# Two blocks on one core: keys' parts share the partitions, splits on VectorE, routing in steps

## The chip, the core and the metric

The kernel runs on one core of a Trainium2 chip. A core has five engines that work at the same time, each through its own list of instructions in a fixed order: TensorE (PE: matrix products; PEld is its loading of the stationary operand), VectorE (DVE), ScalarE (ACT), GpSimd (POOL) and SyncE (SP). SP and POOL also issue DMAs. An instruction waits on semaphores for what it needs, and everything behind it on that engine waits too. The metric is the device time of one execution in microseconds (us); three runs of the kernel before took 2537.84 to 2539.66, median 2538.1.

## The reference

Two blocks follow one another on 1024 rows of width 1024, in float32. The first projects x by a wide matrix and feeds three branches (gated spatial mixing, an S5 state-space scan with parameters computed from small tensors, cross attention to a memory), joins them by an output product and a layer norm. The second makes an RG-LRU recurrence and a differential attention beside one another, then a second memory attention and a mixture of 32 experts, of which each row takes two:

```python
def second_block(x, mem, positions, ...):
    h = rms_norm(x, norm_mix)
    lru_in, lru_gate, q, k, v, g_lru, g_attn = split(h @ w_in)
    y_lru = (gelu(lru_gate) * rg_lru(conv(lru_in))) @ w_lru_o
    # q, k: 8 heads, 2 maps of 64; v: 128 per head; mask by chunks of 64 keys
    q, k = rope(rms_norm(q)) / 8, rope(rms_norm(k))
    sc = einsum('bqhmd,bkhd...->bhmqk', q, k)
    p = softmax(where(mask, sc, -1e30));  w = p[:, :, 0] - lam * p[:, :, 1]
    y_attn = rms_norm(w @ v) @ w_attn_o
    x = x + (sigmoid(g_lru) * y_lru + sigmoid(g_attn) * y_attn) @ w_out
    x = x + memory_cross_attention_2(x, mem)            # 4 heads of 128
    hf = rms_norm(x)                                    # group, then 2 of its 8 experts
    for expert e, rows of it: x += weight * (silu(hf @ gate_e) * (hf @ up_e)) @ down_e
```

## The kernel before, in words

**Products.** A float32 product is made of three matmuls on halves: each operand is split into a rounded high part (`wh`, `xh`, written by ACT, L154) and the rest (`wl`, `xl`, a subtraction on DVE or POOL, L166); `mm3` (L174 to L176) adds high by high, low by high and high by low. Weights come by DMA into `raw`, are split, and are held in rings of two to four buffers.

**Block 1** (`block1`, 0 to about 375 us) begins with eight slices of x (`xraw`, 128x1024 each) and the weight `w_gx`; each slice is split as it lands, most low parts on DVE and every third on POOL, and the first product (tile `pj`) takes one slice after the other. In its own `weights` (L471) the low part goes to POOL. In the same time DVE computes the S5 parameters, a chain of some hundred small instructions (`par_*`, `C`, `S`, `pw`, `ang`). Three lanes, the S5 scan with gating (`left`), the memory attention (`attend`) and the plain projections (`dense`), are merged by a clock of estimated costs.

**Attention** (`attention`, 723 to 1484 us) goes over four pairs of heads. A pair has 16 units: 8 query tiles of 128 rows by 2 heads. For a unit, `unit_qk` makes the scores of both maps in PSUM (`sc`), `unit_mix` the softmax (ACT exponent `e`, DVE), `unit_tr` transposes the weights (`pt<-ident,e`), `unit_pv` multiplies with the values `V`. To keep PE busy, `fill` steps through a generator of other work between units: projections of keys and values (`k_tiles`), of queries (`q_tile`), and gates (`gate_unit`); PSUM products of 24 matmuls of 256 columns. A key tile is normed and rotated (`nr`, on DVE, in a ring of three), twice side by side so that 4 transposes give the same 64 values on both halves of the partitions; `kh` and `kl` are its parts. A query tile `qs` has its high part on partitions 0 to 63 and its low part on 64 to 127, so that one matmul with `kh` and one with `kl` cover all four products. The mask is one more matmul per map, of 256 columns in fp32r (L1482). There is one buffer of `kh`, `kl`, `V`, so at the end of a pair the keys and values of the next are made with no unit beside them (`nxt` stays empty there, and `need` runs the generator).

**Mixer and routing** (`mixer_tiles`, 1642 to 1922 us): the second memory attention in steps s1 to s10 for eight row tiles, each step one tile behind the other; s8 ends x2 and makes the router's rows `h`, s9 transposes them, s10 makes the logits `plg`. `route` chooses experts and fills the lists `lst`, for tiles 0 to 3 early, and for (4, 5, 6) and then (7,) one after the other at the end. A gather of rows by `lsti` starts the experts.

**Experts** (`moe`, 1922 us to the end): PE makes for each expert four groups of 12 matmuls of 512 columns (`pg`, up and gate) and two (`pd`, down), the weights streaming in by DMA, 1 MB each, split in ACT and DVE instructions of 128x2048. `moe_order` and the scheduler set in which order ACT and DVE interleave these with the small steps: `tg` (gating), `xh`, `xl` and `ah`, `al` (inputs of the products), `y` (output, then scattered to memory by POOL, L2213). `beyond`, once, finds the rows that don't fit the 96 of an expert.

Of the kernel before, what the change touches and what calls it, by code (L numbers as in the profile page):

```python
# [30 lines left out]
NY = 3  # L31
# [98 lines left out]
class Model:  # L130
# [321 lines left out]
    def block1(self):  # L452
# [18 lines left out]
        def weights(src, shape, tag, bufs=2, eng=nc.gpsimd):  # L471
# [13 lines left out]
        with tc.high_priority(3 * URGENT):  # L485
            w_gx = weights(A["w_gx"][0], [128, 8, 128], "d", 2, None)
            for k in range(8):
                if 4 <= k < 6:
                    raw = W.tile([128, 1024], F32, name="xraw", tag="wr", bufs=2)
                else:  # L490
                    raw = S5.tile([128, 1024], F32, name="xraw", tag=("u0", "u1", "k", "yt")[k % 4])
# [224 lines left out]
        def attend():  # L716
# [6 lines left out]
            for t in (kph, kpl, vph, vpl):  # L723
                nc.gpsimd.memset(t.bitcast(F32), 0.0)
# [199 lines left out]
        for z in Gx + BT:  # L924
            nc.gpsimd.memset(z.bitcast(F32), 0.0)
# [240 lines left out]
    def attention(self):  # L1166
# [4 lines left out]
        with self.pool("at1") as T1, self.pool("at") as T, \  # L1171
# [16 lines left out]
            ma = T.tile([128, 128], F32R, name="ma")  # L1188
            mb = T.tile([128, 384], F32R, name="mb")
            nc.gpsimd.memset(ma.bitcast(F32), 0.0)  # L1190
            nc.gpsimd.memset(mb.bitcast(F32), 0.0)
            nc.vector.memset(ma.bitcast(F32)[0:1, 0:64], 1.0)
            nc.vector.memset(mb.bitcast(F32)[0:1, 192:256], -(2.0 ** 100))
            self.at = (T, PS, PT, PJ, ma, mb, lamn, sub)

# [24 lines left out]
            def norm_rope(ps, i, is_k):  # L1220

                d = T1.tile([128, 4, 2, 64], F32, name="nr", tag="nr", bufs=3)
# [8 lines left out]
                if is_k:  # L1231
                    self.tt(d, ps[:, :, None, :].to_broadcast([128, 4, 2, 64]),
                            ss[:, 4:8, None, None].to_broadcast([128, 4, 2, 64]), OP.mult)
# [3 lines left out]
                for j in range(2):  # L1237
# [4 lines left out]
                self.tt(d[:, :, :, 0:16], r[:, 0, :, None, :].to_broadcast([128, 4, 2, 16]),  # L1242
                        r[:, 1, :, None, :].to_broadcast([128, 4, 2, 16]), OP.add)
                return d, ss[:, 4:8]

            def transposed(d):
# [1198 lines left out]
```

## Time and profile before

| | |
|---|---|
| median of three runs | 2538.1 us |
| profiled execution | 2542.32 us, of which the span of the trace 2540.4 |
| PE, PEld busy | 2381.8 us (94%), 1966.0 (77%) |
| DVE, ACT, POOL busy | 1775.6 us (70%), 1245.3 (49%), 594.0 (23%) |
| DMA | 394 MB, 155 GB/s over the span, 350 GB/s and more among the experts |

"Busy" counts time in which an instruction of the engine runs. PE's matmuls overlap: one of 512 columns lasts about 400 ns in the record, but the next starts 230 ns later, and one of 256 columns 285 ns with the next 118 ns later; so what a matmul costs is read from start to start. The chain of waits of this profile holds only the last scatter and says nothing of what came before; time is therefore read by stages.

### The profile page before, as it was taken

The numbers are of one execution on the slowest core, as the hardware profiler recorded it, in microseconds if no ns is written. First come the engines' busy times: TensorE is split into PE (matmuls) and PEld (weight loads), VectorE is DVE, ScalarE is ACT, GpSimd is POOL, SyncE is SP. The second block draws the span as 40 slices with busy tenths as digits, with TensorE's granted clock in tenths as the row PEclk, the third lists the DMA queues.
The fourth block names the chain that finished last, engine by engine and source line by source line (L and its number), as shares of the span: only waits on it lengthen the run. The fifth ranks groups of instructions, "written<-read, shape, count | busy, mean of one in ns | idle before, by whom it ended". The sixth has DMA issues, their size and how long they took to land. (4 is left out here: it accounts for less than half of the span.)

```text
span 2540.4 us, 34497 instructions
## 1 busy us (share of the span) xinstructions
PE 2381.8 (94%) x13016; PEld 1966.0 (77%) x13016; DVE 1775.6 (70%) x3153; ACT 1245.3 (49%) x1850; POOL 594.0 (23%) x425
## 2 busy tenths in 40 slices
PE   6999979998989999999999899999988998999997
PEld 5888868777889899898898778887876766766665
DVE  8567677687785676666666743334557998999897
ACT  4354532345455444545454532034435776776665
POOL 4322213222131021021021010001222232333343
PEclk9999989999999999999999999999998999999999
DMA  5322335322121101101110366541247997999995
GB/s 185 116 64 73 115 115 184 121 69 71 65 75 50 55 30 55 63 34 49 52 51 34 110 207 215 176 164 69 84 199 274 374 377 266 349 370 360 350 341 201
DMA packets 104281, 394.28 MB, mean 155 GB/s; under 512 B 14641, under 2 KB 33585, under 8 KB 79537
## 3 DMA queue, kind: packets, MB, share of 16 engines
q1 hardware_dynamic: 85584, 335.41, 37.0%
q0 software_dynamic: 18528, 56.65, 7.1%
q8 instruction: 104, 1.70, 0.3%
q14 instruction: 65, 0.52, 0.1%
HBM read 339.07 MB, written 61.31 MB: 158 GB/s over the span
## 5 line engine op out<-in xcount | busy, mean ns | idle before, releaser
L154 ACT ACTIVATE wh<-raw 128x2048 fp32r<-128x2048 f32 (+2 forms) x310 | 479.7, 1557 | 312.9 <-PE pj L175 82.2
L166 DVE TENSOR_TENSOR wl<-raw,wh 128x2048 fp32r<-128x2048 f32 (+2 forms) x287 | 553.4, 1939 | 96.3 <-ACT wh L154 95.8
L174 PE MATMUL pj<-wh,xnh 128*128 128x256 f32 x768 | 223.1, 290 | 8.9 <-ACT pc L154 4.7
L2213 POOL DMA_INDIRECT out<-y,lsti x32 | 145.9, 4559 | 356.3 <-DVE y L162 343.3
L176 PE MATMUL pj<-wh,xnl 128*128 128x256 f32 x768 | 218.5, 284 | 0.0
L175 PE MATMUL pj<-wl,xnh 128*128 128x256 f32 x768 | 217.8, 284 | 0.0
L175 PE MATMUL pg<-wl,xh 128*96 128x512 f32 x512 | 205.0, 400 | 13.3 <-DVE wl L166 12.6
L176 PE MATMUL pg<-wh,xl 128*96 128x512 f32 x512 | 201.8, 395 | 0.0
L174 PE MATMUL pg<-wh,xh 128*96 128x512 f32 x512 | 200.3, 397 | 0.0
L174 PEld LDWEIGHTS pj<-wh,xnh 128*128 128x128 f32 x768 | 145.8, 190 | 11.9 <-ACT pc L154 6.7
L179 POOL TENSOR_TENSOR ss<-ss,mhalf 128x4 f32<-128x4 f32 (+1 forms) x68 | 74.0, 1088 | 314.2 <-DVE ss L163 222.1
L175 PEld LDWEIGHTS pj<-wl,xnh 128*128 128x128 f32 x768 | 146.6, 191 | 0.0
L176 PEld LDWEIGHTS pj<-wh,xnl 128*128 128x128 f32 x768 | 145.4, 189 | 0.0
L154 ACT ACTIVATE e<-sc,st,ss 128x1024 f32<-128x1024 f32 (+7 forms) x128 | 105.6, 828 | 67.9 <-DVE st L158 50.9
L175 PEld LDWEIGHTS pg<-wl,xh 128*96 128x96 f32 x512 | 82.8, 162 | 55.8 <-DVE wl L166 23.2
L174 PEld LDWEIGHTS pg<-wh,xh 128*96 128x96 f32 x512 | 83.0, 162 | 37.2 <-ACT wh L154 2.2
L174 PE MATMUL pj<-xnh,wh 128*128 128x512 f32 x256 | 103.6, 405 | 5.6 <-ACT wh L154 5.6
L176 PEld LDWEIGHTS pg<-wh,xl 128*96 128x96 f32 x512 | 83.1, 162 | 33.0 <-DVE xl L166 0.2
L174 PE MATMUL pg<-xnh,wh 128*128 128x512 f32 x256 | 103.7, 405 | 0.0
L175 PE MATMUL pg<-xnl,wh 128*128 128x512 f32 x256 | 102.5, 400 | 0.0
L176 PE MATMUL pj<-xnh,wl 128*128 128x512 f32 x256 | 102.4, 401 | 0.0
L176 PE MATMUL pg<-xnh,wl 128*128 128x512 f32 x256 | 102.4, 400 | 0.0
(999 smaller groups left out, 6590.2 us busy)
## 6 DMA issues: line engine op xcount, KB each, us to landing
raw<-in_w_gu SPq DMA_DIRECT2D x128, 1024.0 KB, 9.0
raw<-in_w_dn SPq DMA_DIRECT2D x64, 1024.0 KB, 9.8
raw<-in_w_out SPq DMA_DIRECT2D x16, 512.0 KB, 4.4
ta<-tg POOLq DMA_DIRECT2D x32, 256.0 KB, 2.6
t<-ta SPq DMA_DIRECT2D x14, 512.0 KB, 4.2
raw<-in_w_ga SPq DMA_DIRECT2D x12, 512.0 KB, 3.8
raw<-in_w_v SPq DMA_DIRECT2D x12, 512.0 KB, 3.5
xraw<-in_xT SPq DMA_DIRECT2D x8, 512.0 KB, 6.4
```

What stands on the lines that cost most here:

```text
L154: return self.nc.scalar.activation(out=out, in_=in_, func=func, **kw)
L166: return (eng or self.nc.vector).tensor_tensor(out=out, in0=a, in1=b, op=op)
L174: mm(ps, l[0], r[0], start=start, stop=False)
L175: mm(ps, l[0], r[1], start=False, stop=False)
L176: mm(ps, l[1], r[0], start=False, stop=stop)
L179: self.nc.gpsimd.tensor_tensor(out=out, in0=in_, in1=self.mhalf[:, :w], op=OP.pow)
L2213: return nc.gpsimd.indirect_dma_start(out=self.out, out_offset=bass.IndirectOffsetOnAxis(ap=u["row"], axis=0), in_=u["y"], in_offset=None, ...
```

## The change

**Start.** The first weight and the slices of x get a higher priority than the small parameters; a seventh slice has a buffer of its own; all low parts in block 1 and the clearings of `kph`, `kpl`, `vph`, `vpl`, `Gh`, `Gl`, `Bh` and `Bl` (7424 columns in all) are on DVE, and a few small DMAs move from SP's queue to POOL's.

```diff
-        def weights(src, shape, tag, bufs=2, eng=nc.gpsimd):
+        def weights(src, shape, tag, bufs=2, eng=None):
-        with tc.high_priority(3 * URGENT):
+        with tc.high_priority(5 * URGENT):
-                self.split(xh[:, k], xl[:, k], raw, nc.gpsimd if k % 3 == 2 else None)
+                self.split(xh[:, k], xl[:, k], raw)
...
-                nc.gpsimd.memset(t.bitcast(F32), 0.0)
+                nc.vector.memset(t.bitcast(F32), 0.0)
...
-            nc.sync.dma_start(out=kd[u].rearrange("p g k n -> (p g k) n")[:, 0:7 * 16], in_=pad)
+            nc.gpsimd.dma_start(out=kd[u].rearrange("p g k n -> (p g k) n")[:, 0:7 * 16], in_=pad)
```

SP's list at the start of the kernel before, from its sixth row (`in_xT` are the slices of x, `in_w_gx` the weight, `kd`, `pos`, `lq`, `bc`, `cmat`, `dsk` small tensors; the last three stand ahead of these rows):

```order
L473 DMA raw<-in_w_gx 128x1024
L492 DMA xraw<-in_xT 128x1024 x6
L928 DMA kd_183<-pad 128x112
L928 DMA kd_184<-pad 128x112
L928 DMA kd_185<-pad 128x112
L928 DMA kd_186<-pad 128x112
L374 DMA pos<-in_pos 128x8
L407 DMA lq<-in_lamqk 128x256
L473 DMA raw<-in_w_gx 128x1024
L492 DMA xraw<-in_xT 128x1024 x2
L473 DMA raw<-in_w_xb 128x1024 x2
```

Here four small DMAs and two more stand between the sixth slice and the last two. SP's list after, from its third row:

```order
L473 DMA raw<-in_w_gx 128x1024
L491 DMA xraw<-in_xT 128x1024 x7
L270 DMA bc<-in_s5b 128x256
L272 DMA cmat<-in_s5c 128x256
L922 DMA dsk<-in_ssd 16x16
L374 DMA pos<-in_pos 128x8
L407 DMA lq<-in_lamqk 128x256
L473 DMA raw<-in_w_gx 128x1024
L491 DMA xraw<-in_xT 128x1024
L473 DMA raw<-in_w_xb 128x1024 x2
```

Seven slices now follow the weight directly; the parameters come behind them, and the eighth slice after the second weight.

**Attention.** Keys: the high part of a map lies on one half of the partitions and the low part on the other, in one tile `kk` with two buffers; `qs` holds the high and the low part on both halves. A key tile is no longer doubled, so it takes 2 transposes, not 4 (256 become 192 in all, with the queries'). The mask has 64 columns in bf16. The gates' result `tg` and the attention's output `ot`, which a DMA of POOL's queue stores, had a buffer each and now take theirs from the ring `nr`. The generator makes keys and values of the first pair first; then in each pair the queries and gates, the values `V` of the pair after its second query tile, and the keys of the next pair at its end, and the loop over units no longer stops between pairs.

```diff
-                kh = T.tile([128, 4, 1024], F32R, name="kh", tag="kh")
-                kl = T.tile([128, 4, 1024], F32R, name="kl", tag="kl")
...
+                kk = KV[p] = [T.tile([128, 4, 1024], F32R, name="kk", tag="kk", bufs=2), None]
-                    self.act(kh[:, :, q], pt, AF.Copy, scale=gcol[:, 1:2])
-                    self.stt(kl[:, :, q], pt, gcol[:, 1:2], kh[:, :, q].bitcast(F32), OP.mult, OP.subtract)
+                    for m in range(2):
+                        a, b = slice(64 * m, 64 * m + 64), slice(64 - 64 * m, 128 - 64 * m)
+                        g = gcol[a, 1:2]
+                        self.act(kk[0][a, m:4:2, q], pt[a], AF.Copy, scale=g)
+                        self.stt(kk[0][b, m:4:2, q], pt[a], g, kk[0][a, m:4:2, q].bitcast(F32), OP.mult, OP.subtract)
...
-                t = T.tile([128, 512], F32, name="tg", tag="tg", bufs=1)
+                t = T1.tile([128, 512], F32, name="tg", tag="nr", bufs=3)
...
-                    if q[0] == p:
-                        need(q[0], q[1])
-                        nxt = self.unit_qk(q, QS, KV)
-                        queries(p, n % 16 + 1)
...
+                    need(QS, (q[0], q[1]))
+                    nxt = self.unit_qk(q, QS, KV)
+                    queries(n + 1)
...
+                need(vals, p)
                 for g, tr in zip(G, trs):
...
-                nc.tensor.matmul(base[:, o:o + n], qs[:, a], kh[:, a, k0:k0 + n], start=True, stop=False)
-                nc.tensor.matmul(base[:, o:o + n], qs[:, a], kl[:, a, k0:k0 + n], start=False, stop=not last)
+                for r in range(2):
+                    nc.tensor.matmul(base[:, o:o + n], qs[:, r, a], kk[:, a, k0:k0 + n], start=r == 0,
+                                     stop=r == 1 and not last)
...
-                    nc.tensor.matmul(base[:, o + n - 256:o + n], ma, mb[:, 128:384] if i == 0 else mb[:, 0:256],
-                                     start=False, stop=True)
+                    nc.tensor.matmul(base[:, end - 64:end], ma, mb, start=False, stop=True)
```

ACT's list around the first exponents (`e`) of the second pair, before (`wth`: a unit's transposed weights; `qs`: query tile; `pc`, `nq`, `nr`: a projection and its norm; `tg`: a gate):

```order
L154 ACTIVATE qs<-pt,gcol 128x512
L154 ACTIVATE nq<-pc 128x256
L154 ACTIVATE nr<-pc 128x512
L154 ACTIVATE pc<-pj 128x256
L154 ACTIVATE nq<-pc 128x256
L154 ACTIVATE nr<-pc 128x512
L154 ACTIVATE qs<-pt,gcol 128x512
L154 ACTIVATE e,st<-sc,st,ss 128x128 x2
L154 ACTIVATE tg<-pg 128x512
L154 ACTIVATE wth<-pt 128x128
```

The pair begins with its own queries, and no unit of the pair before is left. The same place after (`V`: values, `osq`: a unit's output):

```order
L154 ACTIVATE qs<-pt,gcol 128x512
L154 ACTIVATE kk<-pt,gcol 64x2x128
L154 ACTIVATE pc<-pj 128x256
L154 ACTIVATE wth<-pt 128x512
L154 ACTIVATE wth<-pt 128x128
L154 ACTIVATE e,st<-sc,st,ss 128x128 x2
L154 ACTIVATE V<-pc 128x2x128 x2
L154 ACTIVATE qs<-pt,gcol 128x512
L154 ACTIVATE wth<-pt 128x128
L154 ACTIVATE osq<-o_7652 128x512
L154 ACTIVATE e,st<-sc,st,ss 128x1024 x2
```

The last unit of the pair before (its `wth` of 512 and 128 columns) stands directly beside the first exponents, and the values follow them.

**Mixer.** The scaling of `on` and the rows `h` go from POOL to DVE, `h` behind s9; the clearing of `xg` too. `route` becomes a generator with three stops, and at the end the batch (4, 5, 6) is routed between the halves of s8 for tile 7.

```diff
+                s7(7)
+                s10(6)
+                r = routes[batches[1]]
+                next(r)
+                s8(7, (0,))
+                next(r)
+                s8(7, (1,))
+                next(r)
+                s9(7)
+                for _ in r:
+                    pass
```

**Experts.** `beyond` uses no POOL; its matmul is made three experts later (`spread` at `OVAT + 3`).

```diff
                 if e == OVAT:
-                    beyond()
+                    over = beyond()
+                if e == OVAT + 3:
+                    spread(*over)
```

With the other moves the scheduler also finds another order among the later experts. ACT's list for one of them before (from the 20th on):

```order
L154 ACTIVATE xh<-pt 128x384 x2
L154 ACTIVATE wh<-raw 128x2048
L154 ACTIVATE tg<-pg,lst 96x512
L154 ACTIVATE wh<-raw 128x2048 x5
L154 ACTIVATE ah<-pt 128x384
L154 ACTIVATE xh<-pt 128x384 x2
L154 ACTIVATE wh<-raw 128x2048
```

Here `tg` is followed by five `wh`. The list after (from the 17th on):

```order
L154 ACTIVATE wh<-raw 128x2048 x3
L154 ACTIVATE tg<-pg,lst 96x512
L154 ACTIVATE wh<-raw 128x2048 x2
L154 ACTIVATE xh<-pt 128x384
L154 ACTIVATE wh<-raw 128x2048
L154 ACTIVATE xh<-pt 128x384
L154 ACTIVATE ah<-pt 128x384
L154 ACTIVATE wh<-raw 128x2048 x3
```

`tg`, which needs PE's second group of `pg`, stood ahead of the last `wh` of that expert's up weights, and now stands behind it; one of the five or six `wh` now lies between the two `xh`. DVE's list for the same experts, before:

```order
L166 TENSOR_TENSOR xl<-pt,xh 128x384 x2
L162 TENSOR_SCALAR y<-pd,lst 96x512
L166 TENSOR_TENSOR wl<-raw,wh 128x2048
L166 TENSOR_TENSOR al<-pt,ah 128x384
L166 TENSOR_TENSOR wl<-raw,wh 128x2048
L158 SCALAR_TENSOR_TENSOR tg<-tg,pg 96x512
L166 TENSOR_TENSOR wl<-raw,wh 128x2048 x2
L166 TENSOR_TENSOR tg<-tg,pg 96x512
L166 TENSOR_TENSOR wl<-raw,wh 128x2048
```

Both `xl` stand together ahead of the expert's second `y`. DVE's list after:

```order
L162 TENSOR_SCALAR y<-pd,lst 96x512
L166 TENSOR_TENSOR xl<-pt,xh 128x384
L166 TENSOR_TENSOR wl<-raw,wh 128x2048
L162 TENSOR_SCALAR y<-pd,lst 96x512
L166 TENSOR_TENSOR xl<-pt,xh 128x384
L166 TENSOR_TENSOR al<-pt,ah 128x384
L166 TENSOR_TENSOR wl<-raw,wh 128x2048 x3
L158 SCALAR_TENSOR_TENSOR tg<-tg,pg 96x512
L166 TENSOR_TENSOR wl<-raw,wh 128x2048
```

The second `y`, which needs the end of the last `pd`, stood ahead of `wl`, `al` and `wl`, with both `xl` done; now one `xl`, `al` and three `wl` wait behind it.

## Rows read from the trace of the kernel before

**Rows 1.** The page's part 1: engine, busy us and share, instructions.
```profile
PE 2381.8 (94%) x13016; PEld 1966.0 (77%) x13016; DVE 1775.6 (70%) x3153; ACT 1245.3 (49%) x1850; POOL 594.0 (23%) x425
```

**Rows 2.** Windows: length, busy us (instructions) of each engine, granted clock, DMA share, GB/s.
```profile
0.00:35.00 35.00, 14.64 (x44) 10.15 (x45) 32.34 (x137) 16.38 (x20) 21.73 (x22) 0.91 0.69 230
35.00:125.00 90.00, 87.21 (x451) 74.05 (x450) 60.04 (x217) 31.79 (x59) 27.99 (x14) 0.98 0.39 123
862.00:913.00 51.00, 44.84 (x267) 39.48 (x266) 34.55 (x84) 23.93 (x50) 5.31 (x6) 0.97 0.17 57
913.00:1044.00 131.00, 130.59 (x943) 122.58 (x942) 83.40 (x219) 67.42 (x142) 23.11 (x26) 1.00 0.14 47
1044.00:1093.00 49.00, 42.95 (x248) 38.13 (x248) 31.35 (x78) 21.04 (x45) 5.38 (x6) 0.94 0.15 49
1880.00:1925.00 45.00, 30.83 (x176) 25.70 (x176) 29.28 (x105) 13.97 (x25) 14.20 (x13) 0.79 0.64 247
```

**Rows 3.** Waits, 14 to 36 us: engine, line, awaited; us, times, longest.
```profile
PE pj L175 <- DVE xl L166: 8.2, 1, 8.2
```

**Rows 4.** Timeline of DVE, 14 to 36 us: start, us, instruction.
```profile
19.12 0.16 DVE L166 TENSOR_TENSOR sca<-sca,par_th 128x8 f32<-128x8 f32 x1
...
20.10 2.34 DVE L166 TENSOR_TENSOR C<-C 128x8 f32<-128x8 f32 x1
...
32.68 1.22 DVE L166 TENSOR_TENSOR xl<-xraw,xh 128x1024 fp32r<-128x1024 f32 x1
```

**Rows 5.** Line L166 until 480 us: ns min/median/max, first and last start.
```profile
L166 POOL TENSOR_TENSOR wl<-raw,wh x23: 2360/2397/2637, 22.4 to 283.4; 128x1024 fp32r<-128x1024 f32 x23
```

**Rows 6.** Line L1482, the mask: ns min/median/max, first and last start.
```profile
L1482 PE MATMUL sc<-mb,ma x128: 276/281/418, 792.8 to 1454.8; 128*128 128x256 f32 x128
```

**Rows 7.** Timelines of PE at 955, 1769 and 1843 us: start, us, instruction.
```profile
955.30 0.60 PE L1249 MATMUL pt<-ident,nr 128*128 128x128 f32 x4
955.65 0.37 PE L174 MATMUL pj<-wh,xnh 128*128 128x256 f32 x1
955.86 0.28 PE L175 MATMUL pj<-wl,xnh 128*128 128x256 f32 x1
...
1769.06 1.87 PE L1973 MATMUL plg<-wrt,hT 128*128 128x36 f32 x16
...
1843.53 0.18 PE L2062 MATMUL prk<-rt_M,tri 128*128 128x32 bf16 x1
1843.55 0.23 PE L2064 MATMUL prk<-rt_M,one 128*128 128x32 bf16 x3
```

**Rows 8.** Timelines of PE and DVE at the mixer's end; in brackets idle before, releaser.
```profile
1894.83 0.63 PE L1856 MATMUL ptr<-ident,on 128*128 128x128 f32 x4 [2.52 <-DVE on L166]
...
1908.07 2.45 PE L1973 MATMUL plg<-wrt,hT 128*128 128x36 f32 x16 [2.33 <-DVE hT L1960]
...
1904.78 2.30 DVE L166 TENSOR_TENSOR cacc<-cacc,rt_M 128x32 bf16<-128x32 bf16 x1
```

**Rows 9.** Timeline of PE at 2102 us, and of POOL's scatters, one per expert.
```profile
2102.47 0.62 PE L2256 MATMUL po<-ovd,ov 22*128 22x44 f32 x2 [9.02 <-DVE ovd L162]
...
2067.40 3.23 POOL L2213 DMA_INDIRECT out<-y,lsti  x1 [11.31 <-DVE y L162]
...
2085.09 3.24 POOL L2213 DMA_INDIRECT out<-y,lsti  x1 [11.09 <-DVE y L162]
...
2114.72 3.23 POOL L2213 DMA_INDIRECT out<-y,lsti  x1 [8.26 <-DVE y L162]
...
2273.12 5.90 POOL L2213 DMA_INDIRECT out<-y,lsti  x1 [10.61 <-DVE y L162]
...
2488.06 8.08 POOL L2213 DMA_INDIRECT out<-y,lsti  x1 [9.85 <-DVE y L162]
```

**Rows 10.** Waits, 2260 to 2460 us, as in group 3.
```profile
ACT tg L154 <- PE pg L176: 34.3, 11, 3.8
```

**Rows 11.** The page's part 6: DMA, times, KB each, median us to landing.
```profile
ta<-tg POOLq DMA_DIRECT2D x32, 256.0 KB, 2.6
```

More of the change, by code (lines that the diff above doesn't have):

```diff
@@ L1220, in norm_rope @@
             def norm_rope(ps, i, is_k):
-                d = T1.tile([128, 4, 2, 64], F32, name="nr", tag="nr", bufs=3)
+                w = 1 if is_k else 2
+                d = T1.tile([128, 4, w, 64], F32, name="nr", tag="nr", bufs=3)
                 sq = T0.tile([128, 4, 64], F32, name="nq", tag="nq", bufs=1)
@@ L1300, in k_tiles, with v_tiles @@
                         pend.append((n, d))
-                    if n == 1:
-                        yield "v", p
+                    if n == 4:
+                        WQ[p] = w2(A["w_q2"][p])
                     if n > 1:
-                        j = n - 2
-                        o = []
-                        yield from proj(wv, j, o)
-                        ps = o[0].rearrange("p (h a) b -> p h (a b)", h=2)
-                        self.split(V[:, j, :, 0], V[:, j, :, 1], ps)
-                        finish()
-                        yield 0.3
-                        if j == 3:
-                            WQ[p] = w2(A["w_q2"][p])
+                        finish()
+                        yield 0.2
+            def v_tiles(p):
+                wv = WV.pop(p)
+                V = KV[p][1] = T.tile([128, 8, 2, 2, 128], F32R, name="V", tag="V")
+                for j in range(8):
+                    o = []
+                    yield from proj(wv, j, o)
+                    ps = o[0].rearrange("p (h a) b -> p h (a b)", h=2)
+                    self.split(V[:, j, :, 0], V[:, j, :, 1], ps)
+                    if j == 7:
+                        vals.add(p)
+                    yield 0.1
             def q_tile(p, i):
@@ L1382, in attention, with need @@
             tail, early = [], []
-            def need(p, i):
+            def need(what, key):
                 alone[0] = True
                 n = 0
-                while (p, i) not in QS:
+                while key not in what:
                     if step() is None:
@@ L1397, in attention, with queries @@
             o4 = {}
-            done.update({("k", 0), ("v", 0)})
-            def queries(p, u):
-                for m in range(8):
+            def queries(u):
+                for m in range(32):
                     t = m + 1 - QB
-                    if m == 7 or t < 0 or 4 * (t // 2) + 2 + t % 2 <= u:
-                        done.add(("q", p, m))
-            queries(0, 0)
-            need(0, 7)
+                    if t < 0 or 4 * (t // 2) + 2 + t % 2 <= u:
+                        done.add(("q", *divmod(m, 8)))
+            queries(0)
+            need(QS, (0, 7))
             cur = self.unit_qk(units[0], QS, KV)
@@ L1761, in mixer @@
         nc.vector.memset(self.cacc, 0.0)
+        self.iop = self.const.tile([NOV, 2], F32, name="iop")
+        nc.gpsimd.iota(self.iop, pattern=[[1, 2]], base=0, channel_multiplier=1, allow_small_or_imprecise_dtypes=True)
         self.brow = self.row(C, "b_rt", 36)
@@ L1936, in s7, with s8 @@
             S[i]["o"] = oh, ol
-        def s8(i):
+        def s8(i, halves=(0, 1)):
             oh, ol = S[i]["o"]
-            ps = P2.tile([128, 2, 512], F32, name="pw", tag="po")
-            for n in range(2):
+            if 0 in halves:
+                S[i]["pw"] = P2.tile([128, 2, 512], F32, name="pw", tag="po")
+            ps = S[i]["pw"]
+            for n in halves:
                 for k in range(4):
@@ L2254, in beyond, with spread @@
                 self.ts(d[:, 1], self.ident[0:NOV, 0:NOV], r[:, 2:3], OP.mult)
+                nc.vector.tensor_copy(out=res[:, 1, 0:1], in_=ov[0:1, 1, 31:32])
+                return one, d
+            def spread(one, d):
                 po = PT.tile([128, 2, NOV], F32, name="po", tag="pt")
```

127 lines of the change are left out of this document (69 added, 58 removed).

## The prediction

> **What bounds the kernel now.** I read the shares first: PE is busy 94% of the span [rows 1], so what isn't PE's own work can give back at most the 159 us that it idles, and less PE work counts in full only where nothing else is late. Then the windows by stage. In the middle of a pair of heads PE idles 0.41 of 131 us; from one pair to the next it idles 6.16 of 51 and 6.05 of 49 [rows 2], and the third such place is like the second. The first 35 us hold 14.64 us of PE, the last 45 of the mixer 30.83 [rows 2]. The waits name what is late there: at the start one wait of 8.2 us for a low part of x from DVE [rows 3], at the mixer's end `on` and `hT` from DVE [rows 8], among the experts one gap of 9.02 us for `ovd` [rows 9], and late ACT's `tg` waiting for PE [rows 10]. So the change is a sum of places, not a new bound.
>
> **Start.** DVE is busy 32.34 of 35 us [rows 2], but part of that is standing still: a product of 8 columns lasts 2.34 us at 20.10, as long as one split on POOL (2.40) [rows 4, 5]. The last low part of x begins only at 32.68 [rows 4], behind parameters. In the changed kernel the slices go first and no split runs on POOL; each costs DVE 1.22 us [rows 4]. PE then follows the loads. I give back 8 us of the 8.2; the bounds are 0 (the slices land no earlier than PE ends now) and 12 (POOL's stretch goes too). It carries on only if what follows can move up: from 35 to 125 us PE is busy 87.21 of 90, DVE 60.04 [rows 2], so PE sets the pace and DVE has 30 us for the parameters that now come later.
>
> **The splits of block 1.** 25 move: 25 x 1.22 = 31 us more on DVE, and clearings of 7424 columns, at most 7.25 x 1.22 = 9 if a column costs what it does in the split. Against this, each of 23 POOL splits can have held a DVE instruction for 2.34 - 0.16 = 2.2 us (0.16 is the product of 8 columns at 19.12, beside no POOL work [rows 4]), so up to 50 us of standing still goes. Net DVE time lies between +40 and -50; most sits beside PE work with the free 30 us as cover. On the path I take 0, with bounds of 8 either way, as large as the start's wait: without that cover `pj` would wait for a `wl` again.
>
> The row of 2.34 us bears on who holds whom. The Trainium skill (SBUF — State Buffer, "Who interferes with whom") says that a DVE instruction with two SBUF inputs and a GpSimd one that reads SBUF exclude one another for a whole instruction, which the row agrees with, but that a GpSimd instruction that only writes doesn't disturb it. By that, the clearings' move is price alone; with all 9 us of it on the path the time would be 2496.
>
> **Attention, between pairs.** 6.16 + 6.05 + 6.05 = 18.3 us of idle PE stand at the three places where a pair ends. The changed loop makes the next pair's scores while the last unit's `wth` and its product with V are still to come, so PE has work where it waited for the first exponents. The cover is now those products and 8 tiles of V, each 24 x 118 ns = 2.8 us. If it isn't enough, the next thing late is V's weights. I take 15 of 18.3; bounds 0 and 18.3.
>
> **Attention, transposes.** Four take from 955.30 to the second matmul behind them at 955.86, less one matmul of 118 ns: 0.44 us, 0.11 each [rows 7]. 64 fewer: 7.0 us, on PE, which is bound here. ACT and DVE work on a key tile is cut in two halves of the partitions with the same columns in all, and one norm on DVE halves; ACT is busy 67 and DVE 83 of 131 us [rows 2], so I count nothing; without this cover the 32 more instructions on ACT and 32 on DVE, at 0.16 us or somewhat more each [rows 4], would cost 10.
>
> **Attention, mask.** 128 matmuls [rows 6] shrink from 256 to 64 columns. The low bound of the new one is 25 ns: two more `prk` of 32 bf16 columns lengthen the record from 0.18 to 0.23 us [rows 7]; that gives 128 x 93 ns = 12 us. The other: `plg` has 36 columns and a new float32 stationary each time, and 16 take 1.87 us, 117 ns each [rows 7], no less than 256 columns take. Behind a mask comes again a matmul with new fp32r weights, so I go with the latter: 1 us, bounds 0 and 12.
>
> The Trainium skill (TensorE: Matmul & The Clock Gate) has both: "Back-to-back issue gap" puts up to 64 columns at an issue floor of about 25 ns, "LDWEIGHTS" the load of 128 columns at 107 ns. `prk` agrees with the first, `plg` with the second. By the first the time would be 2476, by the second it is the sum here.
>
> **Mixer.** The row of 2.52 us is the wait for `on`, that of 2.33 us for `hT`, behind a `cacc` of 2.30 us with a POOL multiplication running [rows 8]; a product of 8 columns beside no POOL work takes 0.16 [rows 4], so some 2 us of it is standing still. Routing (4, 5, 6) inside step 9 takes two thirds of the serial lists from the end, some 4 us of the 14.2 that PE idles in these 45 us [rows 2]. 2 + 2 + 4 = 8, and 1 for the clock: 0.79 granted in this window [rows 2], where the same 16 `plg` last 2.45 us against 1.87 [rows 7, 8]. The three clearings of `xg` now on DVE (3072 columns, at most 3.7 us) lie beside it. 9 us, bounds 3 and 13.
>
> **Experts, `beyond`.** One scatter comes 29.63 us after the one before, where 17.69 is usual [rows 9]: 11.94 us lost. PE no longer waits, but DVE still has the chain ahead of its splits and must catch up. I take 8; bounds 4 and 12.
>
> **Experts, the order.** From 2273.12 to 2488.06 there are 11 experts [rows 9], 19.54 us each: 11 x 1.85 = 20.4 us above the usual. The reason is ACT's `tg`, ahead of a `wh`, waiting 34.3 us in 11 times for PE [rows 10], 3.1 each. In the new order `tg` stands behind that `wh`, so this goes; but on DVE the second `y`, which waits for PE's last `pd`, has three `wl` behind it, and 14 experts are of that kind. No row shows it. Bounds: no loss (+20) and 1.85 each (14 x 1.85 = 26, that is -5.5). I take two thirds of the old loss, 14 x 1.24 = 17.4, so +3.
>
> **Sum.** 8 + 0 + 15 + 7 + 1 + 9 + 8 + 3 = 51. The profiled execution takes 2542.3 us, so 2491.3 there; the median of the runs is 4.2 lower, so 2487.
>
> **The rivals.**
> - *V is late at a pair's beginning.* V's weights get their ring buffers only when the last key projection is done, and `need` then holds PE until load and split end. For it: weights pass a load, an ACT and a DVE split, and nothing but two query tiles (5.6 us) is in between. Against: the raw loads can run ahead. If each place keeps its 6 us, 15 are gone: 2502.
> - *The new expert order is no better than the old.* For: DVE's `y` before three `wl`. Against: `tg` is out of ACT's way. At -5.5 for +3: 2496; were all at 20.1 us, as single ones before are, 14 x 2.4 = 34, that is -13: 2503.
> - *The mask at 25 ns*, by the rule above: 2476. For it `prk`; against it `plg`, which is nearer (float32 weights next).
> - *All ends well*: start 12, pairs 18, mixer 13, `beyond` 12, order 15: 78 us, 2460.
> - *Slower: the ring `nr` blocks.* Gates and outputs now take their buffers from the ring of three that DVE's norms use. A buffer is free when its DMA has landed, 2.6 us [rows 11]; 32 gates and 16 outputs make 48. If DVE's next `nr` waits for that, everything behind it on DVE waits, the softmax too. Twenty waits in full (52 us) eat the sum; from there on the kernel is slower, and with forty (104 us) it takes 2591. Against: between two allocations lies at least one projection of 2.8 us, longer than the landing.
>
> **Chances.** Forecast 0.55, its own range 2472 to 2502; V late 0.12; order no better 0.12; mask or all well 0.12; ring 0.06; no effect in sum (the parameters become late and eat the start, others halve) 0.03. About 0.2% (5 us) is what a measurement can tell from no change. Faster than that: 0.55 + 0.12 + 0.12 + 0.12 less 0.05 for several misses together = 0.86; same 0.05; slower 0.09. The range 2452 to 2518 takes in all cases but the ring and the worst sums.
>
> **What would show it.** Right: the first `pj` group ends near 25 us; no gap above 2 us at the three pair ends; 192 `nr` transposes, mask spacing about 110 ns; no gap at `po`; scatters of the late experts 18.5 to 19.3 us apart. Wrong: a wait of PE for `V` or `wl` at the pair ends, DVE's `nr` waiting for a DMA, PE waiting for `Gh` near 55 us, or late scatters 20 us apart.

## The result: slower by 0.56%

The changed kernel takes 2552.0 us (median of five runs, 2550.4 to 2553.4) against 2538.1: a ratio of 1.0056, with a 95% interval of 1.0043 to 1.0070. The forecast was 2487, so the direction was wrong. The profiled execution takes 2550.72 us, its span is 2548.9, 8.5 more than before. The profiled execution before was 4.2 above its median, so the stages below add up to about 9 us and not to the 13.9 by which the medians differ.

| stage, us (read from PE's starts) | before | after | gain | forecast |
|---|---|---|---|---|
| to the first mask of the attention | 792.8 | 769.2 | +23.6 | +8 |
| first mask to the last `pj` of the output product | 848.7 | 873.3 | -24.6 | +23 |
| from there to `pcn`, which ends the lists | 278.6 | 277.2 | +1.4 | +9 |
| `pcn` to the first `pg` of the experts | 6.0 | 9.5 | -3.5 | 0 |
| first `pg` to the last `pd` | 601.0 | 607.0 | -6.0 | +11 |

The start gave three times what was forecast, and the attention took all of it back before the mixer began. The shares of the span [rows 1] show nothing of this; PE is even busy 9 us less.

```profile
PE 2372.9 (93%) x12952; PEld 1942.8 (76%) x12952; DVE 1782.2 (70%) x3240; ACT 1253.0 (49%) x1882; POOL 549.0 (22%) x375
```

The windows do; columns as in [rows 2], on the clock of the changed kernel, where a stretch of the attention begins some 23 us sooner (1122 and 2260 us are two more places):

```profile
0.00:35.00 35.00, 24.52 (x95) 19.61 (x96) 31.59 (x106) 21.43 (x27) 11.16 (x15) 1.00 0.85 288
35.00:125.00 90.00, 90.00 (x488) 77.14 (x487) 67.86 (x284) 37.17 (x68) 3.86 (x3) 1.00 0.36 110
862.00:913.00 51.00, 44.04 (x309) 40.45 (x308) 35.12 (x105) 24.04 (x53) 11.39 (x13) 0.90 0.09 32
913.00:1044.00 131.00, 124.60 (x848) 111.12 (x848) 82.03 (x211) 66.86 (x143) 16.45 (x19) 1.00 0.15 49
1122.00:1132.00 10.00, 7.09 (x32) 6.20 (x32) 6.45 (x15) 2.77 (x5) 1.01 (x1) 0.68 0.01 2
1880.00:1925.00 45.00, 31.47 (x171) 26.62 (x169) 29.81 (x111) 13.03 (x23) 8.13 (x7) 0.73 0.63 242
2260.00:2460.00 200.00, 178.81 (x829) 122.31 (x828) 171.86 (x130) 129.94 (x100) 107.95 (x21) 1.00 0.97 336
```

The first 35 us hold 24.52 us of PE, not 14.64, and the 90 after them are full. In the stretch with the end of the first pair (862 to 913 us) PE idles 6.96 of 51 us, still. And the 131 us that held 0.41 of idle time now hold 6.40, of which 3.8 are a second stall, at the beginning of a pair; at 1122 us, in the next pair, it also takes the granted clock to 0.68. PE's timeline at that second stall, at a pair's end and at the end of the attention (idle before an instruction and its releaser in brackets):

```profile
1125.17 0.38 PE L1538 MATMUL po<-V,wtl 128*128 128x256 f32 x1 [1.52 <-DVE wtl L166]
1126.57 0.58 PE L174 MATMUL pj<-wh,xnh 128*128 128x256 f32 x1 [1.01 <-ACT e L154]
...
1247.47 0.73 PE L1491 MATMUL sc<-kk,qs 128*128 128x512 f32 x2 [1.30 <-ACT e L154]
1248.05 0.20 PE L1496 MATMUL sc<-mb,ma 128*128 128x64 bf16 x1
1248.09 0.71 PE L1491 MATMUL sc<-kk,qs 128*128 128x512 f32 x2
...
1252.21 1.33 PE L1525 MATMUL pt<-ident,e 128*128 128x128 f32 x5 [2.46 <-DVE e L158]
...
1254.41 0.28 PE L1496 MATMUL sc<-mb,ma 128*128 128x64 bf16 x1
...
1433.35 1.22 PE L1491 MATMUL sc<-kk,qs 128*128 128x512 f32 x2 [3.33 <-ACT e L154]
...
1439.75 1.43 PE L1491 MATMUL sc<-kk,qs 128*128 128x320 f32 x4 [2.71 <-ACT e L154]
```

At 1247 and 1252 us PE waits 1.30 and 2.46 us for exponents `e` of the last units of the same pair: the pair's last mask follows at 1254.41, and the first mask of the next pair comes only at 1299.3. The kernel before has the same two waits in the same place, ahead of the last mask of a pair (912.04), and as good as no idle time from there to the first mask of the next pair (972.0); its timeline and, in the form of [rows 2], its windows to either side of that last mask:

```profile
905.06 0.50 PE L1479 MATMUL sc<-kh,qs 128*128 128x512 f32 x1 [1.14 <-ACT e L154]
...
909.85 1.33 PE L1512 MATMUL pt<-ident,e 128*128 128x128 f32 x5 [2.44 <-DVE e L158]
...
912.04 0.42 PE L1482 MATMUL sc<-mb,ma 128*128 128x256 f32 x1
```
```profile
862.00:912.00 50.00, 43.84 (x262) 38.68 (x261) 33.55 (x81) 23.30 (x49) 5.31 (x6) 0.97 0.17 58
912.00:972.00 60.00, 59.96 (x502) 59.53 (x502) 39.43 (x106) 30.55 (x64) 14.80 (x16) 0.99 0.16 54
```

So the 6.16 us [rows 2] lie among a pair's last units and not between two pairs. In the changed kernel, at 1126 us, a *projection* (`pj`) waits for ACT's `e`, since it writes a buffer of the scores. From 1433 us on nothing is left to fill the last units' waits.

At the mixer's end PE waits as follows; DVE's list ahead of the first wait stands below it:

```profile
1894.67 1.08 PE L1871 MATMUL ptr<-ident,on 128*128 128x128 f32 x4 [3.53 <-DVE on L166]
...
1907.78 3.63 PE L1996 MATMUL plg<-wrt,hT 128*128 128x36 f32 x16 [1.34 <-DVE rs L163]
...
1923.65 1.54 PE L2209 MATMUL pt<-ident,xg 96*128 96x96 f32 x8 [3.80 <-DMA xg<-x3d,lsti]
...
1928.58 0.90 PE L2209 MATMUL pt<-ident,xg 96*128 96x96 f32 x4 [3.40 <-DMA xg<-x3d,lsti]
```
```profile
1889.47 1.23 DVE L1942 TENSOR_REDUCE on<-po 128x512 f32<-128x1024 f32 x1 [0.19 <-PE po L1940]
1890.85 0.91 DVE L2035 MEMSET xg<- 96x1024 f32 x1 [0.16 <-issue]
1891.92 0.91 DVE L2035 MEMSET xg<- 96x1024 f32 x1 [0.16 <-issue]
1893.00 0.91 DVE L2035 MEMSET xg<- 96x1024 f32 x1 [0.16 <-issue]
...
1893.85 0.67 DVE L166 TENSOR_TENSOR on<-on,st 128x512 f32<-128x512 f32 x1
```

The three clearings of `xg`, counted beside the path, stand between `on`'s reduction and its scaling, and the wait grows from 2.52 [rows 8] to 3.53 us. The 16 `plg` take 3.63 us where they took 2.45, in a window with 0.73 of the clock. The two waits for the gathered rows `xg` were 3.29 and 0.45 us before; it is the second that grew.

Among the experts these are the scatters (one each) and the waits from 2260 to 2460 us, to be set against [rows 9, 10]:

```profile
2088.93 3.34 POOL L2252 DMA_INDIRECT out<-y,lsti  x1 [11.40 <-DVE ov L158]
2106.82 3.34 POOL L2252 DMA_INDIRECT out<-y,lsti  x1 [11.32 <-DVE ov L158]
...
2194.01 3.24 POOL L2252 DMA_INDIRECT out<-y,lsti  x1 [9.88 <-DVE y L162]
...
2477.09 8.56 POOL L2252 DMA_INDIRECT out<-y,lsti  x1 [11.70 <-DVE y L162]
```
```profile
ACT xh L154 <- PE pt L2209: 45.4, 10, 4.5
PEld pg L175 <- DVE wl L166: 30.4, 20, 2.1
PE pg L175 <- DVE wl L166: 21.2, 20, 1.6
ACT tg L154 <- PE pg L176: 18.6, 10, 1.9
```

The place that took 29.63 us (`beyond`) takes 17.89. But the 14 experts from 2194.01 on take 20.22 each, and ACT waits 45.4 us for the transposes of x (`xh`), `tg`'s wait having fallen from 34.3 to 18.6.

### The profile page after: what moved, and what is told of

It reads as the page before. It is cut to its first block, busy times and chain, and to the rows that moved or that the text cites. A ratio compares the mean times of both kernels' runs of the same rounds, so it can differ in the third digit from the quotient of the medians.

```text
span 2548.9 us, 34475 instructions
## 1 busy us (share of the span) xinstructions
PE 2372.9 (93%) x12952; PEld 1942.8 (76%) x12952; DVE 1782.2 (70%) x3240; ACT 1253.0 (49%) x1882; POOL 549.0 (22%) x375
## 5 line engine op out<-in xcount | busy, mean ns | idle before, releaser
L166 DVE TENSOR_TENSOR wl<-raw,wh 128x2048 fp32r<-128x2048 f32 (+2 forms) x310 | 580.7, 1887 | 116.6 <-ACT wh L154 115.9
L2252 POOL DMA_INDIRECT out<-y,lsti x32 | 175.2, 5475 | 331.3 <-DVE y L162 281.4
L1491 PE MATMUL sc<-kk,qs 128*128 128x512 f32 (+4 forms) x384 | 99.5, 373 | 15.6 <-ACT e L154 10.2
L174 PEld LDWEIGHTS pg<-wh,xh 128*96 128x96 f32 x512 | 83.1, 162 | 37.4 <-ACT wh L154 1.4
L175 PE MATMUL pj<-xnl,wh 128*128 128x512 f32 x256 | 101.7, 397 | 0.0
```

Of the source, the lines that this page charges most:

```text
L166: return (eng or self.nc.vector).tensor_tensor(out=out, in0=a, in1=b, op=op)
L174: mm(ps, l[0], r[0], start=start, stop=False)
L175: mm(ps, l[0], r[1], start=False, stop=False)
L1491: nc.tensor.matmul(base[:, o:o + n], qs[:, r, a], kk[:, a, k0:k0 + n], start=r == 0, stop=r == 1 and not last)
L2252: return nc.gpsimd.indirect_dma_start(out=self.out, out_offset=bass.IndirectOffsetOnAxis(ap=u["row"], axis=0), in_=u["y"], in_offset=None, ...
```

## The experiments

Each result gives the median time in us, its ratio to the kernel before and the 95% interval of the ratio; the kernel before ran at 2538.0 to 2540.1 beside them. "Attention" is the stretch of the table's second line, "first mask" the start of the first one. Each version is scheduled anew, so an edit can also move other work.

**The start alone**: the diff's hunks of the start, put into the kernel before.

> The kernel before with the start and block 1 of the changed kernel alone (loads first, low parts and clearings on DVE). In the changed kernel's trace the first mask of the attention comes at 769.2 us, 23.6 earlier than before. Theory: this is the start part's work alone, and nothing later takes it back, since the rest is the kernel before word for word: 2538 - 23 = about 2515. Rival 1: the 23.6 us need the later parts too, or a wait of attention, mixer or experts takes most of it back: 2527 to 2538. Rival 2 (the prediction's own size, 8 us): 2530.

2523.9, ratio 0.9941 [0.9922, 0.9960]; first mask at 772.9, attention 849.8. The gain of the start is real: the first mask comes 19.9 us sooner, and the whole takes 14.2 us less.

**The old attention loop**: the changed kernel with the generator and loop of before; keys in one tile, mask and transposes as changed. Gates and outputs (`tg`, `ot`) have buffers of their own again, so the loop and the ring `nr` are tried together.

```diff
-                    need(QS, (q[0], q[1]))
-                    nxt = self.unit_qk(q, QS, KV)
-                    queries(n + 1)
+                    if q[0] == p:
+                        need(q[0], q[1])
+                        nxt = self.unit_qk(q, QS, KV)
+                        queries(p, n % 16 + 1)
+                    else:
+                        done.add(("k", p + 1))
```

> The changed kernel with the attention's loop as before (keys and values of a pair at its beginning, no unit beside them, gates and outputs in buffers of their own), but with the new layout of keys, the 64-column mask and fewer transposes. Theory (the loop's new order costs): from the first mask to the last matmul of the output product the kernel before takes 849 us and the changed one 873; here the order of before less 64 transposes of 0.11 us, so 841 to 843, and the whole 2552 - 31 = about 2521. Rival (the layout costs: halves of the partitions, the mask with its own weights): the stage stays near 873 and the whole within 5 us of 2552. The late experts stay at 20.3 us apart by either.

2514.1, 0.9895 [0.9878, 0.9911]; attention 837.2. So the new loop, with the ring, costs 36.1 us: 15.2 up to the last mask (671.8 against 656.6) and 20.9 behind it (201.5 against 180.6). Its own trace shows what the new loop did not remove:

```profile
1231.80 0.72 PE L1483 MATMUL sc<-kk,qs 128*128 128x512 f32 x2 [1.33 <-ACT e L154]
1236.53 1.33 PE L1517 MATMUL pt<-ident,e 128*128 128x128 f32 x5 [2.45 <-DVE e L158]
```

These are the same two waits at the pair's end, to 0.03 us. The new loop left them as they were and added others.

**The experts' order**: `xh`, `xl` are held behind the third split of the up weights, `tg` behind the fourth.

```diff
-                        x_parts(U[e + 1])
+                        with tc.issue_after(self.last[0].ins), tc.issue_after(self.last[1].ins):
+                            x_parts(U[e + 1])
-                    gated(u)
+                    with tc.issue_after(self.last[0].ins), tc.issue_after(self.last[1].ins):
+                        gated(u)
```

> The changed kernel with one thing held: among the experts, ACT and DVE make both inputs' parts (xh, xl) of the next expert behind the third split of the up weights, and tg behind the fourth, as in the first twelve experts. Theory (the order alone makes the late experts slow): from the 15th on the scatters come 17.7 us apart and not 20.3, 14 x 2.6 = 36 us less: about 2516. Rival 1 (the loads limit the late experts, 336 GB/s at a DMA share of 0.97): the scatters stay above 19 us apart, 2538 or more. Rival 2 (DVE's share of instructions limits): 18.5 to 19, about 2530.

2539.1, 1.0001 [0.9992, 1.0011]: 13 us less than the changed kernel; the late experts take 19.4 us. `xh` no longer waits, but the next one in ACT's queue does:

```profile
ACT ah L154 <- PE pd L175: 39.7, 9, 4.4
```

**Both**: old loop and held `xh`, `tg`.

> The two edits of the runs before together: the attention's loop as before with the new layout, and the experts' order held; start, mixer and the rest as in the changed kernel. If both theories hold and add up: 2552 - 31 - 36 = about 2485, faster than both kernels. If loads limit the experts or the layout costs, 2515 or more.

2502.0, 0.9849 [0.9832, 0.9865]: the two add up (12.0 and 37.0).

**`ah`, `al` held too**, behind the third split:

```diff
-                    a_parts(v)
+                    ap = a_parts(v)
...
+                    with tc.issue_after(self.last[0].ins), tc.issue_after(self.last[1].ins):
+                        if v:
+                            ap()
```

> As the run e4 (old loop of the attention with the new layout, xl, xh and tg held behind the third and fourth up split), and also ah and al held behind the third up split, as they stand in the first twelve experts. In e4 the late scatters are 19.4 us apart and ACT waits 4.4 us per expert with ah for TensorE, with two wh behind it. Theory (what stands in front of a waiting instruction sets the late experts' pace): 17.7 us apart, 14 x 1.7 = 24 less: 2502 - 24 = about 2478. Rival (loads: DMA share 0.98 and 351 GB/s in e4's late experts, so they can't come faster): 19.0 or more apart, above 2495.

2483.8, 0.9782 [0.9766, 0.9798]; late experts at 18.2. From 2260 to 2460 us PE has hardly any idle time left (it was busy 178.81 of 200 in the changed kernel):

```profile
2260.00:2460.00 200.00, 199.53 (x922) 135.88 (x921) 189.99 (x143) 144.40 (x113) 101.68 (x18) 1.00 0.97 357
```

So the place of `xh`, `tg` and `ah` in ACT's and DVE's queues is worth 31 us (12.9 and 18.2).

**Without the mixer's part**: the last version, mixer and routing as before.

> As e5, but the mixer and the routing as in the kernel before. In the changed kernel's trace the mixer takes 277 us against 279, but the first product of the experts comes 9.5 us behind the last list against 6.0. Theory (the mixer's part brings nothing): within 3 us of e5. Rival (the prediction's 9 us): 9 slower than e5.

2482.3, 0.9764 [0.9748, 0.9780]: the mixer's part, the stepwise routing with it, is worth nothing. Without it the mixer takes 278.6 against 277.6 us, but `pcn` to `pg` 6.1 against 9.7.

**The long mask** in the same version: `ma` and `mb` in fp32r, 256 columns.

> As e5, but the mask again with 256 columns in fp32r. Theory (the next weights set the mask's cost, as the 36-column products show with 117 ns): within 2 us of e5. Rival (25 ns each for the short mask): 12 us slower than e5.

2496.8, 0.9822 [0.9804, 0.9840]: 13.0 us more, attention 848.4 against 834.8. So the version with the short mask is 13 us faster, not 1; but the scheduler also places the other work differently. With the long mask PE idles 33.3 us of the attention, with the short one 26.3; the last matmul of the gates starts at 1405.8 and not 1386.9, and 24 of the 96 early matmuls of the output product lie ahead of the last mask, not 48.

**The loads alone**: the kernel before with the priority, the seventh buffer and `kd` on POOL's queue, splits on POOL as they were.

> The kernel before with only the loads of the start reordered (weight and x first, seventh slice in a buffer of its own, small DMAs of kd on POOL's queue); low parts and clearings stay on POOL as before. e1, with those moved too, takes 2524 against 2538. Theory (POOL's work beside DVE costs what moving it costs, so the loads are the gain): 2524 to 2528. Rival (the moved splits are the gain, since DVE stands still beside POOL): 2533 or more.

2542.5, 1.0013 [1.0003, 1.0022]: no gain, first mask at 791.3. The first 35 us hold 19.79 us of PE where the kernel before has 14.64, but the next 90 hold 81.47 where it has 87.21. DVE's timeline has a split of 6.67 us in place of 1.22, while POOL makes two splits from 14.97 to 19.66:

```profile
14.08 6.67 DVE L166 TENSOR_TENSOR xl<-xraw,xh 128x1024 fp32r<-128x1024 f32 x1 [0.57 <-ACT xh L154]
```

**The splits alone**: the kernel before, low parts and clearings on DVE, loads as they were.

```diff
-                self.split(xh[:, k], xl[:, k], raw, nc.gpsimd if k % 3 == 2 else None)
+                self.split(xh[:, k], xl[:, k], raw)
```

> The kernel before with only the low parts and clearings of block 1 moved from POOL to DVE; the order of the loads as before. e1 (both) took 2524, e8 (the loads alone) 2542, before 2538 to 2540. Theory (POOL's work beside DVE is what costs): 2523 to 2528. Rival (only both together give it, since DVE's parameters otherwise stand ahead of the last slices): 2532 or more.

2522.2, 0.9938 [0.9921, 0.9955]; first mask at 773.0. The two windows become those of the changed kernel with the loads in their old order:

```profile
0.00:35.00 35.00, 23.97 (x93) 18.69 (x94) 31.14 (x98) 20.21 (x22) 8.97 (x10) 1.00 0.81 284
35.00:125.00 90.00, 90.00 (x485) 77.00 (x484) 67.94 (x293) 38.07 (x73) 3.86 (x3) 1.00 0.36 111
```

The moved splits (with the clearings) are all of the gain that the start brings by itself: DVE is 8 us *more* busy in the 90, and PE never waits. Another 3.7 of the table's 23.6 us came with the other parts; no run tells with which.

**The second stall** (on the version with held `xh`, `tg`, 2539.1, as the next three): V's projections, called for by `need(vals, p)`, no longer take the scores' buffers.

```diff
-                alone[0] = True
+                alone[0] = what is QS
```

> As the run e3 (the changed kernel with its new attention loop, experts partly held, 2539 us), but the projections of V that a unit waits for take the PSUM buffers of the projections, not those of the scores. In the changed kernel's trace the first of them waits 1.0 us for an exponent at 1126.6, and PE idles 2.9 of 10 us there at a granted clock of 0.68. Theory (the next unit's scores hold the buffers that V's projections want): at each pair's beginning 3 to 4 us less, 2539 - 10 = about 2529. Rival (the stall is the last unit's own chain of transposes and products with V, without other work beside it): within 3 us of 2539.

2533.7, 0.9979 [0.9969, 0.9988]: most of the stall at 1125 us goes, 5.4 us where 10 were expected. From the first mask of a pair to that of its 12th unit PE idles 2.3 to 2.7 us, where it was 4.5 in each of the last three pairs.

**The keys earlier**: the next pair's key tiles ahead of the last two gates.

> As e3, but in the order of other work the keys of the next pair stand ahead of the last two gates of a pair, so that projections lie between the last units. In e3 PE idles 1.3 and 2.5 us before the last units of each pair, as in the kernel before. Theory (nothing is left to fill the last units): 2 to 4 us less per pair, about 2530. Rival (the scheduler places the same work after the units anyway, since the weights come late): within 3 us of 2539.

2534.7, 0.9986 [0.9977, 0.9996]: 4.4 us. The gaps of 1.30 and 2.46 at the end of the third pair become 0.61 and, ahead of a projection, 0.65, but gaps of 2.8 and 2.9 come in the keys' own block.

**The hold**: the wait on a pair's last query tile moved behind gates and keys.

```diff
-                        yield "q", p, n
+                        if n < 7:
+                            yield "q", p, n
...
+                    yield "q", p, 7
```

> The version with the held x and gating (2539.1), and the wait on a pair's last query tile moved behind the last two gates and the next pair's keys, as in the kernel before, where the eighth tile is never held. Theory (the fillers stand still at a pair's end because of that hold): the gaps of 1 to 3 us at the pair ends and the 8 us more of idle PE before the output product go, -15 to -25 us, about 2519; the first early output product starts within 5 us of the last gate, not 26. Rival (the pair ends are dear because the scores of the next pair wait for their own queries): no more than the 4.4 us that the earlier keys gave, 2535 or above.

2540.3, 1.0005 [0.9995, 1.0014]: no gain, and the gaps are the same ones, so the theory of the hold fell. The first early output product starts 27 us after the last matmul of the gates (1449.1 and 1422.2 us), where it was to start within 5.

**Hold and buffers**: the last edit together with that of the second stall.

> The same, and V's projections no longer in the scores' buffers. If hold and buffers are the whole price of the new loop: 2502 to 2506, the time of the version with the old loop (2502.0). If a third cause is left, 2510 or more, about 5 below the run with the hold alone.

2534.1, 0.9981 [0.9972, 0.9991]: the buffers' 5 us again (2539.1 without both edits). A third cause is left.

**The same and `ah` held**: these two edits, with `ah` and `al` behind the third split as well.

> The same, and the inputs of the second expert product held behind the third split of the up weights too. The old loop with that stands at 2483.8. If the new loop's idea (scores of the next pair beside the end of this one) is worth something once its holds are gone: below 2480; if it is worth nothing: 2484 to 2488; if a price is left: above 2490.

2514.0, 0.9902 [0.9886, 0.9919], against 2483.8 with the old loop: 30 us of the new loop's price are left.

**No cover behind the last gate**: the version with the old loop and held `ah` (2483.8), with the early output products put back into the output product itself.

```diff
-N0 = 2
+N0 = 0
```

The reason to try it are the starts of these products, first and last, in the changed kernel and in the one with the old loop (form of [rows 6]):

```profile
L174 PE MATMUL po<-b00h,wh x4: 477/630/774, 1449.2 to 1478.9; 128*128 128x512 f32 x4
```
```profile
L174 PE MATMUL po<-b00h,wh x4: 473/476/505, 1392.4 to 1435.5; 128*128 128x512 f32 x4
```

With the old loop they begin 34 us ahead of the last mask (1426.8) and half of them lie between the last units; with the new one they begin 8 us behind it (1441.0).

> The best version with the old loop (2483.8), with the 96 matmuls of the output product that run beside the last attention units put back into the output product itself (same work, other place). If the lost cover is what the new loop pays after the last mask: the stretch from there to the output product's end grows from 180.4 us to about 200, the time to 2495 or more. If the place of these products is indifferent: 195 or less for the stretch (the part that stood before the last mask, 48 x 0.23 = 11 us, moves behind it, and the masks come that much sooner), 2484 to 2488.

2501.5, 0.9854 [0.9838, 0.9871]: 17.7 us slower; from the last mask to the output product's end 196.8 us instead of 180.4, and no mask comes sooner. From 1380 to 1420 us, without and with the early products:

```profile
1380.00:1420.00 40.00, 28.24 (x136) 21.80 (x134) 29.25 (x55) 21.03 (x36) 1.08 (x2) 0.75 0.46 158
```
```profile
1380.00:1420.00 40.00, 33.32 (x164) 25.39 (x163) 30.56 (x58) 22.50 (x39) 2.31 (x4) 0.91 0.44 152
```

Without them PE idles 5 us more in these 40, and the rest runs at 0.75 of the clock rather than 0.91. The 16.4 us are near the 20.9 that the new loop pays behind the last mask.

## Why the prediction was wrong, step by step

**Start** (+8; the place measured 23.6): the mechanism was half right and the term mis-sized. I gave the gain to the loads; alone they give nothing, the splits alone 16 us of time and 19.8 by the first mask.

**The splits of block 1** (0, range ±8): the net effect of moved price and ended standing still is this gain. I had the 50 us of standing still in the text and took 0, reasoning from DVE's free time; but DVE's spare time says nothing of when a split is ready. The gain grows as long as the old kernel's splits on POOL last (22 to 283 us [rows 5]): the first product with `Gh` comes 4.4 us sooner (62.5, 58.1), the last `pv` 15.2 (345.1, 329.9). With no split of block 1 on POOL, DVE's products of 8 columns take 0.16 to 0.18 us in the changed kernel, and none 2.34 (min/median/max in ns, as in [rows 5]):

```profile
L166 DVE TENSOR_TENSOR C<-C x9: 163/166/178, 37.6 to 46.6; 128x8 f32<-128x8 f32 x9
```

This agrees with the rule of the Trainium skill (SBUF — State Buffer, "Who interferes with whom") that the prediction weighed. The rule's other half, on instructions that only write, would make the clearings' move pure price; the runs move both together, so it isn't shown.

**Attention, between pairs** (+15): **this step failed, in its place and in its sign.** It took the idle PE at the three pair ends for a wait for the next pair's first exponents, and gave it the last unit's `wth` and product with V as cover. The order showed these side by side, but there was nothing to cover: from a pair's last mask to the next pair's first PE was busy 59.96 of 60 us. The idle time lies ahead of the last mask, where the last units wait for their own exponents. The scores of the next pair come behind it, so the new loop could not fill it, and the waits of 1.30 and 2.46 us are still there. Nor are the 131 us with 0.41 of idle time the middle of a pair: they are the way from one pair to the next and the beginning of the next.

What I did not price was the other end of the move: V's projections were cover *between* pairs and are now forced inside the pair, where they (a) take buffers of the scores, which wait for `e` (5.4 us), and (b) push the gates back. The last matmul of the gates starts 18.1 us ahead of the last mask (1422.9, 1441.0), with the old loop 37.4 ahead (1389.4, 1426.8), so the early output products come too late to cover the last units (16.4 of 20.9 us by the last run). With the keys' 4.4 this makes 26 of 36 us, if they add up, which no run tries.

By place, PE idles 26.6 us more than with the old loop (53.2 against 26.6): 12.6 from the first mask of a pair to that of its 12th unit, 5.7 between pairs, 1.6 in the last units, 6.6 behind the last mask. The other 9.5 are longer busy time for the same 4994 matmuls: behind such gaps the granted clock stands at 0.50 (1.2 of 2.4 GHz), for 51.2 us of the stretch, with the old loop for 30.7. These 20.5 us more at half the rate make about 10, by my estimate. That (b) is what the missing cover comes from is read from the two traces, and its price from the last run; no run puts the cover back into the new loop, none parts the loop from the ring `nr`, and some 10 us of the price are open.

**Transposes and mask** (+7 and +1): the old loop with both gains 11.5 us in the attention. With the transposes and the long mask the attention takes 848.4 us, with the start alone 849.8, so of the transposes' 7 little is left beside the halved copies; they were not tried alone. The mask's term was too small: the short mask's version is 13.0 us faster. I took `plg` as its model because float32 weights follow; the rival with 25 ns and 12 us was nearer in its number, but its mechanism isn't shown. From start to start the 128 masks take 7.0 us in place of 17.0, the 384 `sc` beside them 79.9 in place of 76.4. So about half of the 13 us is PE's own work, and the other half is the 7.0 us of idle time by which the two versions differ; how much of that the other order of work brings is open. The prediction's reading by the Trainium skill (TensorE: Matmul & The Clock Gate, "Back-to-back issue gap"), an issue floor of about 25 ns, the trace bears out in part: the next matmul starts 40 ns behind a short mask (1248.05, 1248.09) and 110 to 120 behind a long one, but the two `sc` ahead of the second mask there take 0.54 us, with the long one 0.47, and the whole group of two masks takes 1.39 us with either.

**Mixer** (+9): failed. 1.4 us were gained in the mixer, and 3.5 lost behind `pcn`, where PE waits 3.80 and 3.40 us for the gathers of `xg` (3.29 and 0.45 before); with the old mixer the loss is gone, but which of its moves delays the second gather is open. The clearings that were to lie beside the path are on it, and DVE, now with POOL's work, is as busy as before in these 45 us (29.81 against 29.28).

**Experts, `beyond`** (+8): right, with 11.7 measured within the bounds of 4 and 12.

**Experts, the order** (+3): **failed too.** 18.9 us were estimated for each of 14 experts, 20.2 came. That is 35 us above 17.7 each, against the old order's 20.4, a term of -15. My reason for a price, DVE's second `y`, is not what the trace names. ACT's `xh` waits 4.5 us per expert for PE's transposes, with `wh` behind it, and PE then waits for `wl`. Holding `xh`, `tg` and `ah` back gives 31 us. A rival had this place with at most -13.

**The ring `nr`**, the only rival on the slow side, did not happen: no `nr`, `tg` or `ot` waits for a DMA in the attention. The kernel became slower by two steps that I had read from the order of the lists; I gave 0.09 to that side. And it is luck that the version with the old loop and the held order, 2483.8, stands near the forecast of 2487: by the table's stages it gains 23.6, 13.8, 1.0, -3.7 and 24.6 us, where 8, 23, 9, 0 and 11 were forecast.

## What to carry to other kernels

A window that holds idle time does not tell what waits in it: before crediting a cover, find the instruction behind each gap and the unit to which it belongs, and set the start of the cover against the start of the gap. Then follow what leaves its old place to whatever it displaces, down to the last consumer of the cover. In a full queue a single small instruction that waits for another engine costs something in every round: here 0.8 and 1.2 us per expert, 31 us in all, for `xh`, `tg` and `ah`, less than the 4.5 and 4.4 that they wait. A split on POOL was not free for DVE, though POOL had time to spare: moving 25 of them and the clearings to the busier DVE gave 16 us.

## Not expected of the hardware

A split of 1.22 us on DVE lasted 6.67 while POOL made two splits (the loads-only run). PE's gaps came with a lower clock behind them: 28.24 us of work in 40 ran at a mean granted clock of 0.75, 33.32 at 0.91; and behind the gap of 2.46 us at 1252.21 the `pj` of 256 columns start 0.21 us apart at 0.50, a few us later 0.12 at 1.00. And 128 masks of 64 bf16 columns took 10 us less from start to start than 128 of 256 in fp32r, but the `sc` beside them 3.5 us more.
